# Streamed weights in two rings of buffers: six places for the split parts and four for the raw tiles, instead of five and six

## The chip, the cores and the metric

The kernel runs on one core of a Trainium2 chip. The metric is the device time of one execution in microseconds. The kernel computes in single precision on a batch of one with 256 tokens of width 1024, and it reads every weight matrix once from memory.

## The reference, cut to what matters

The reference is a network of two blocks on x of shape (1, 256, 1024). Every matrix product below is done with streamed weights, and these products are nearly all the work.

```python
# first block, layer 0: retention, 4 heads, chunks of 128
z = rms_norm(x) @ ret_w_in                  # 1024 x 6144: q, k, v, gate
o = retention(rope(q), rope(k), v)
y = (silu(gate) * rms(o)) @ ret_w_out       # 2048 x 1024
x = x + rms_norm(y);  x = x + (p[0] @ ple_w_proj[0]) * sigmoid(x @ ple_w_gate[0])
# layer 1: latent attention, 16 heads
z = rms_norm(x) @ mla_w_in                  # c_q, c_kv, k_rope, gate
s = softmax(causal(q(c_q @ w_uq) . k(c_kv @ w_uk, k_rope)))
y = (silu(gate) * (s @ (c_kv @ w_uv))) @ mla_w_out
x = x + rms_norm(y);  x = x + (p[1] @ ple_w_proj[1]) * sigmoid(x @ ple_w_gate[1])
# second block: convolution and pooling branches, then a gated feed-forward
mod = silu(c) @ w_ada + b_ada               # 1024 x 6144, on VectorE
h = layer_norm(x) * (1 + sc1) + sh1;  proj = h @ w_in
mix = (sig(gate_a) * branch_a + sig(gate_b) * branch_b) @ w_out
x = layer_norm(ALPHA * x + g1 * mix)
up = causal_dwconv((layer_norm(x) * (1 + sc2) + sh2) @ w_up)   # 1024 x 5632
x = layer_norm(ALPHA * x + g2 * (gelu(gt) * v) @ w_down)       # 2816 x 1024
```

## The kernel before, in words

All activations stay in the core's memory, transposed, with the 256 tokens as the columns of a matmul. Weights are packed ahead of time into 258 tiles of 128 x 1024 single-precision numbers (512 KB), in the order in which the program asks for them, and streamed.

**A split tile.** TensorE takes single precision at full speed only in a reduced form, so most tiles are split in two. `fetch` (L157) issues the load of a raw tile on SP's queue. `load` (L170) casts it on ScalarE into a high part (L178, tag `wh`) and subtracts that from the raw tile on VectorE, which gives the low part (L179, tag `wl`). `mm` (L236) then makes each product of three matmuls: high by high (L237), high by low (L238) and low by high (L239). A tile of 1024 columns holds eight 128-column weight blocks, or two 512-column ones where the weights are the moving operand (the value projections and the down projection).

**A plain tile.** In four places of the second block the raw tile goes to TensorE as it is, in full precision (`mm32`, L242, with its matmul on L243). `fetch` puts such a tile into a raw buffer or into a `wh` buffer, by the parity of its number. The first tile of the program is a plain one too.

**The rings.** The pool `wp` has three tags: `raw`, `wh` and `wl`. A buffer of a tag is free when the last instruction that uses its tile has ended: for a raw tile that is the subtraction on VectorE, for the parts the last matmul. A load waits on SP for a free raw buffer, a cast on ScalarE for a free `wh` buffer, a subtraction on VectorE for a free `wl` one. The scheduler of the kernel language gives out the buffers when the program is built, orders each engine's instructions by its own estimate of when they can run, and sets the waits; on the chip each engine keeps that order.

**The order of work.** `Seq` (L144) walks a list of weight blocks and calls `load` whenever a new tile begins. In the attention layer four such sequences are open at a time (`seq_g`, `seq_q`, `seq_k`, `seq_v`: gates, queries, keys, values), so that tiles of them can be half used at a time. Side work is put into the matmul stream by a clock that counts matmul columns (`tick`, `after`): softmax, normalisation, the convolution, and `ada` (L413), the 48 products that make `mod`, whose 512 KB tiles are loaded on SP's queue as well, behind one another in program order. `keep_in_program_order` is also set for the loads of the first tiles.

Of the kernel before, what the change touches and what calls it, by code (L numbers as in the profile page):

```python
# [12 lines left out]
F32R = mybir.dt.float32r  # L13
# [6 lines left out]
P = 128  # L20
S = 256
D = 1024
# [60 lines left out]
def tile_kernel(ctx, tc, order, xT, pT, pos, vec, cst, cv, rows, wada, wts, outT):  # L83
# [5 lines left out]
    wp = ctx.enter_context(tc.tile_pool(name="wp", bufs=5))  # L89
# [7 lines left out]
    def nm(s):  # L97
        uid[0] += 1
        return f"{s}_{uid[0]}"
# [44 lines left out]
    class Seq:  # L144
# [3 lines left out]
        def next(self):  # L148
            per = D // self.w
            s = self.i % per  # L150
            if s == 0:
                self.h, self.l = load(self.e[self.i:self.i + per], self.w, self.parts, self.ready.pop(0) if self.ready else None)
            self.i += 1
            sl = slice(s * self.w, (s + 1) * self.w)
            return self.h[:, sl], self.l[:, sl]

    def fetch(entries, width, parts=True, step=D, pinned=False):  # L157
        g = len(order)
        order.append((width, list(entries)))
        n = len(entries) * width  # L160
        tag, bufs = (("raw", 6), ("wh", 5), ("wl", 5))[0 if parts else [0, 1][g % len([0, 1])]]
        raw = wp.tile([P, D], F32, tag=tag, name=nm("raw"), bufs=bufs)
        for o in range(0, n, step):
            e = min(n, o + step)
            d = nc.sync.dma_start(out=raw[:, o:e], in_=wts[g, :, o:e])
            if pinned:
                tc.keep_in_program_order(d)
        return raw[:, :n]

    def load(entries, width, parts=True, raw=None):  # L170
        if raw is None:
            raw = fetch(entries, width, parts)
        if not parts:
            return raw, raw
        n = raw.shape[1]
        hi = wp.tile([P, D], F32R, tag="wh", name=nm("wh"), bufs=5)[:, :n]
        lo = wp.tile([P, D], F32R, tag="wl", name=nm("wl"), bufs=5)[:, :n]
        A.copy(hi, raw)  # L178
        V.tensor_sub(lo, raw, hi.bitcast(F32))  # L179
        return hi, lo  # L180
# [81 lines left out]
    for q in range(3):  # L262
        v0raw.append(fetch(v0[2 * q:2 * q + 2], 512, q >= 1, 512 if q == 0 else D, True))
        if q < 2:
            load_x(q + 1)
        if q == 1:
            load_x(3)
# [135 lines left out]
    def ada_steps():  # L403
        def fetch(n):
            ch = sp.tile([P, D], F32, tag="ada1", name=nm("adach"), bufs=2)
            tc.keep_in_program_order(nc.sync.dma_start(out=ch, in_=wada[n * P:(n + 1) * P, :]))
            return ch

        have = [fetch(0), fetch(1)]
        yield  # L410
        for n in range(48):
            ch = have.pop(0)
            V.tensor_tensor_reduce(ch, ch, sc, 1.0, 0.0, MUL, ADD, mod[:, n:n + 1])  # L413
            if n + 2 < 48:
                have.append(fetch(n + 2))
            if n % 8 == 7:
                m = slice(n - 7, n + 1)
                V.tensor_add(mod[:, m], mod[:, m], col("b_ada_2", n - 7, 8))
            yield
# [1087 lines left out]
```

## Time and profile before

| what | value |
|---|---|
| three runs | 850.41, 846.5, 850.07 us; median 850.07 |
| profiled execution, own time | 847.85 us |
| its span, first to last instruction | 846.1 us |
| TensorE busy | 826.1 us (98%), 6114 matmuls |
| VectorE busy | 703.1 us (83%) |
| ScalarE busy | 555.2 us (66%) |
| memory read | 165.41 MB, 197 GB/s over the span |
| mean granted TensorE clock | 0.997 |

Times are in microseconds unless marked ns. A matmul's busy time overlaps that of the next one, so a group's sum can exceed the span. A wait is put down to whoever ended it last. Engines are named PE (TensorE), PEld (its weight loads), DVE (VectorE), ACT (ScalarE), POOL (GpSimd) and SP (SyncE); a small q behind a name is the engine's sequencer, which issues DMAs.

### The profile page before, as it was taken

The page shows a single profiled execution, that of the slowest core. Times are in us where ns is not written, and L with a number is a line of the kernel's source. Part 1 is how long each engine was busy: PE and PEld are TensorE (multiplying, and loading weights), DVE is VectorE, ACT ScalarE, POOL GpSimd, SP SyncE. Part 2 cuts the span into 40 slices and gives each one's busy share as a digit, 9 for nine tenths or more (in the row PEclk, how much of TensorE's full clock was granted, in tenths as well). Part 3 has the DMA queues.
Part 4 walks back from the last instruction along what each step waited for, and adds up shares of the span by engine and source line. Part 5 has one row for each costly group of instructions (what it writes and reads, how often), then busy time and mean ns, then how long its engine had stood idle before and what let it go on. Part 6 is the DMA issues. An engine that isn't in the chain of part 4 may idle for free.

```text
span 846.1 us, 15771 instructions
## 1 busy us (share of the span) xinstructions
PE 826.1 (98%) x6114; PEld 787.9 (93%) x6114; DVE 703.1 (83%) x1283; ACT 555.2 (66%) x968; POOL 9.9 (1%) x30
## 2 busy tenths in 40 slices
PE   8999999999999999998999999999999999999995
PEld 6989999999999989998999999999998999999885
DVE  6999798988889978688874768899677888889986
ACT  7655565545676686777754857999756576666550
POOL 0000000000000000000000000000000000000001
PEclk9999999999999999999999999999999999999998
DMA  9875567778556637374255364245463455567722
GB/s 335 323 258 212 215 217 269 255 264 319 171 182 248 223 145 259 116 263 145 99 184 176 121 224 152 98 150 199 148 224 128 134 190 191 184 214 255 277 77 75
DMA packets 46634, 167.48 MB, mean 198 GB/s; under 512 B 5216, under 2 KB 5472, under 8 KB 46560
## 3 DMA queue, kind: packets, MB, share of 16 engines
q1 hardware_dynamic: 45936, 164.38, 55.1%
q0 software_dynamic: 624, 2.10, 0.9%
q8 instruction: 48, 0.79, 0.4%
q14 instruction: 26, 0.21, 0.1%
HBM read 165.41 MB, written 1.05 MB: 197 GB/s over the span
## 4 chain that ended last, share of the span: by engine, by line
PE 50%; DVE 2%; ACT 1%; issue 1%; DVEq 0%
PE ps L238 13%; PE ps L237 13%; PE ps L239 13%; PE ps L243 10%; PE ps L341 1%; PE ps L363 0%; DVE wl L179 0%; PE ps L920 0%; PE ps L1170 0%; DVE t L1434 0%; DVE sm L1415 0%; DVE half L690 0%; DVE t L1411 0%; DVE t L1412 0%; PE ps L1407 0%
## 5 line engine op out<-in xcount | busy, mean ns | idle before, releaser
L237 PE MATMUL ps<-half,wh 128*128 128x256 f32 x1504 | 425.4, 284 | 1.4 <-ACT half L187 1.4
L238 PE MATMUL ps<-half,wh 128*128 128x256 f32 x1504 | 423.8, 282 | 0.6 <-DVE half L188 0.5
L239 PE MATMUL ps<-half,wl 128*128 128x256 f32 x1504 | 422.0, 281 | 1.1 <-DVE wl L179 1.0
L178 ACT CAST wh<-raw 128x1024 fp32r<-128x1024 f32 x233 | 243.5, 1049 | 154.9 <-PE ps L238 94.8
L179 DVE TENSOR_TENSOR wl<-raw,wh 128x1024 fp32r<-128x1024 f32 x233 | 282.7, 1219 | 59.5 <-ACT wh L178 57.3
L239 PEld LDWEIGHTS ps<-half,wl 128*128 128x128 f32 x1504 | 283.8, 189 | 1.7 <-DVE wl L179 1.7
L238 PEld LDWEIGHTS ps<-half,wh 128*128 128x128 f32 x1504 | 283.4, 188 | 1.9 <-DVE half L188 1.0
L237 PEld LDWEIGHTS ps<-half,wh 128*128 128x128 f32 x1504 | 282.5, 188 | 2.6 <-ACT half L187 2.0
L243 PE MATMUL ps<-half,raw 128*128 128x256 f32 (+2 forms) x384 | 84.9, 380 | 0.0
L243 PEld LDWEIGHTS ps<-half,raw 128*128 128x128 f32 x384 | 72.5, 190 | 10.0
L237 PE MATMUL ps<-wh,half 128*128 128x512 f32 (+1 forms) x202 | 72.6, 360 | 0.9 <-ACT wh L178 0.9
L413 DVE CUSTOM_DVE_ANT_0 adach<-adach,siluc 128x1024 f32<-128x1024 f32 x48 | 58.4, 1218 | 16.7 <-DMA adach<-in_wada 16.7
L238 PE MATMUL ps<-wl,half 128*128 128x512 f32 (+1 forms) x202 | 71.0, 351 | 0.5 <-DVE wl L179 0.5
L239 PE MATMUL ps<-wh,half 128*128 128x512 f32 (+1 forms) x202 | 71.0, 352 | 0.0
L1087 ACT ACTIVATE t<-apad,vec 128x256 f32<-128x256 f32 x106 | 44.3, 501 | 0.5 <-DVE half L1088 0.5
L237 PEld LDWEIGHTS ps<-wh,half 128*128 128x128 f32 x202 | 37.9, 188 | 6.8 <-ACT wh L178 1.7
L238 PEld LDWEIGHTS ps<-wl,half 128*128 128x128 f32 x202 | 38.1, 189 | 6.0 <-DVE wl L179 1.0
L239 PEld LDWEIGHTS ps<-wh,half 128*128 128x128 f32 x202 | 38.0, 188 | 5.6
L1088 DVE TENSOR_TENSOR half<-half,t 128x512 f32<-128x512 f32 x53 | 36.5, 689 | 3.7 <-ACT t L1087 1.8
L187 ACT CAST half<-t 128x256 fp32r<-128x256 f32 (+1 forms) x47 | 20.3, 453 | 17.9 <-DVE t L1347 10.9
L188 DVE TENSOR_TENSOR half<-t,half 128x256 fp32r<-128x256 f32 (+1 forms) x47 | 21.7, 482 | 4.5 <-ACT half L187 3.6
L1342 ACT ACTIVATE t<-ps,vec 128x256 f32<-128x256 f32 x38 | 21.0, 558 | 2.0 <-PE ps L239 1.2
(290 smaller groups left out, 908.1 us busy)
## 6 DMA issues: line engine op xcount, KB each, us to landing
raw<-in_wts SPq DMA_DIRECT2D x257, 512.0 KB, 4.1
adach<-in_wada SPq DMA_DIRECT2D x48, 512.0 KB, 5.0
half<-in_xT SPq DMA_DIRECT2D x4, 256.0 KB, 5.7
half<-in_rows POOLq DMA_DIRECT2D x2, 512.0 KB, 4.7
out<-t SPq DMA_DIRECT2D x4, 256.0 KB, 2.0
cst<-in_cst SPq DMA_DIRECT2D x1, 928.0 KB, 10.6
raw<-in_wts SPq DMA_DIRECT2D x2, 256.0 KB, 4.4
siluc<-in_cv SPq DMA_DIRECT2D x1, 512.0 KB, 9.0
```

The source lines that it names most:

```text
L178: A.copy(hi, raw)
L179: V.tensor_sub(lo, raw, hi.bitcast(F32))
L187: A.copy(hi, src)
L188: V.tensor_sub(lo, src, hi.bitcast(F32))
L237: T.matmul(ps, l[0], r[0], start=first, stop=False)
L238: T.matmul(ps, l[0], r[1], start=False, stop=False)
L239: T.matmul(ps, l[1], r[0], start=False, stop=last)
L243: T.matmul(ps, w, r, start=first, stop=last)
L413: V.tensor_tensor_reduce(ch, ch, sc, 1.0, 0.0, MUL, ADD, mod[:, n:n + 1])
L1087: A.activation(t[:, b, :], apad[:, i0 + b, k:k + S], AF.Copy, scale=w[b])
L1088: V.tensor_add(acc.pair(i0 // 2), acc.pair(i0 // 2), t)
L1342: A.activation(t[:, b, :], ps[:, b, :], AF.Identity, bias=col("b_dw_f_2", m), scale=w[2])
```

## The change

The numbers of buffers of the three tags are changed, in the two functions where they stand: `raw` from 6 to 4, `wh` and `wl` from 5 to 6 each. The sum stays 16 tiles. Nothing else is edited.

```diff
-        tag, bufs = (("raw", 6), ("wh", 5), ("wl", 5))[0 if parts else [0, 1][g % len([0, 1])]]
+        tag, bufs = (("raw", 4), ("wh", 6), ("wl", 6))[0 if parts else [0, 1][g % len([0, 1])]]
         raw = wp.tile([P, D], F32, tag=tag, name=nm("raw"), bufs=bufs)
...
-        hi = wp.tile([P, D], F32R, tag="wh", name=nm("wh"), bufs=5)[:, :n]
-        lo = wp.tile([P, D], F32R, tag="wl", name=nm("wl"), bufs=5)[:, :n]
+        hi = wp.tile([P, D], F32R, tag="wh", name=nm("wh"), bufs=6)[:, :n]
+        lo = wp.tile([P, D], F32R, tag="wl", name=nm("wl"), bufs=6)[:, :n]
         A.copy(hi, raw)
         V.tensor_sub(lo, raw, hi.bitcast(F32))
```

## Rows read from the trace of the kernel before

**Rows 1.** The page, part 1: busy us, share of the span, instructions

```profile
PE 826.1 (98%) x6114; PEld 787.9 (93%) x6114; DVE 703.1 (83%) x1283; ACT 555.2 (66%) x968; POOL 9.9 (1%) x30
```

**Rows 2.** Windows: stretch, length, busy us (instructions) by engine, clock, DMA share, GB/s

```profile
20.00:40.00 20.00, 20.00 (x163) 19.64 (x162) 19.93 (x38) 13.26 (x17) 0.00 (x0) 1.00 0.88 335
...
700.00:720.00 20.00, 20.00 (x172) 20.00 (x171) 17.05 (x29) 12.85 (x21) 0.00 (x0) 1.00 0.52 185
```

**Rows 3.** Waits of PE, whole span: us in total, times, longest

```profile
PE ps L920 <- DVE sm L909: 2.8, 3, 1.7
...
PE ps L239 <- DVE wl L179: 1.0, 2, 0.7
...
PE ps L237 <- ACT wh L178: 0.9, 1, 0.9
...
PE ps L238 <- DVE wl L179: 0.5, 1, 0.5
...
PE ps L363 <- DVE t L300: 0.2, 1, 0.2
```

**Rows 4.** Waits of SP's queue, whole span

```profile
SPq L165 <- DVE wl L179: 380.4, 148, 11.6
```

**Rows 5.** Waits of ACT, whole span

```profile
ACT wh L178 <- PE ps L238: 94.8, 75, 5.0
```

**Rows 6.** Groups by line: shapes, count, busy us, mean ns, idle before, releasers

```profile
L179 DVE TENSOR_TENSOR wl<-raw,wh 128x1024 fp32r<-128x1024 f32 x233 | 282.7, 1219 | 59.5 <-ACT wh L178 57.3
...
L178 ACT CAST wh<-raw 128x1024 fp32r<-128x1024 f32 x233 | 243.5, 1049 | 154.9 <-PE ps L238 94.8 <-issue 28.1 <-PE ps L239 23.3
```

**Rows 7.** Timelines of ACT, DVE and PE near 305 us: start, us, what, [idle before]

```profile
302.71 1.03 ACT L178 CAST wh<-raw 128x1024 fp32r<-128x1024 f32 x1
...
303.77 1.23 DVE L179 TENSOR_TENSOR wl<-raw,wh 128x1024 fp32r<-128x1024 f32 x1 [0.19 <-ACT wh L178]
...
305.06 0.39 PE L239 MATMUL ps<-half,wl 128*128 128x256 f32 x1 [0.73 <-DVE wl L179]
...
308.40 0.39 PE L239 MATMUL ps<-half,wl 128*128 128x256 f32 x1 [0.24 <-DVE wl L179]
```

**Rows 8.** Waits of the weight loads, 296 to 318 us

```profile
PEld ps L239 <- DVE wl L179: 1.4, 2, 0.9
```

**Rows 9.** The raw tiles, 680 to 760 us: idle before them, landing time

```profile
  PE ps L238: 17.0, 15
...
DMA to landing us min/median/max: 3.3/3.5/4.3
```

**Rows 10.** The raw tiles, 0 to 45 us

```profile
DMA to landing us min/median/max: 3.8/6.9/10.9
```

**Rows 11.** Timelines of SP, ACT and DVE near the start

```profile
9.12 1.05 SPq L165 DMA_DIRECT2D raw<-in_wts  x2
...
14.26 1.05 ACT L178 CAST wh<-raw 128x1024 fp32r<-128x1024 f32 x1 [0.45 <-DMA raw<-in_wts]
...
14.43 1.22 DVE L179 TENSOR_TENSOR wl<-raw,wh 128x1024 fp32r<-128x1024 f32 x1
```

**Rows 12.** The raw tiles, 176 to 212 us

```profile
L179 DVE TENSOR_TENSOR wl<-raw,wh x13: 1215/1217/1226, 180.8 to 209.3; 128x1024 fp32r<-128x1024 f32 x13
...
  DMA raw<-in_wts: 2.9, 2
...
DMA to landing us min/median/max: 4.1/5.4/7.1
```

**Rows 13.** The chain of waits: the longest run of plain matmuls

```profile
533.21 27.63 PE ps L243 x128
```

**Rows 14.** Timeline of ACT at 388 us

```profile
388.76 1.05 ACT L178 CAST wh<-raw 128x1024 fp32r<-128x1024 f32 x1 [1.98 <-issue]
```

**Rows 15.** Windows, seven stretches of 20 us from 260 to 400: their sum

```profile
sum 140.00, PE 133.84 PEld 131.25 DVE 116.33 ACT 102.99 POOL 0.20; mean PE 19.12 PEld 18.75 DVE 16.62 ACT 14.71 POOL 0.03
```

## The prediction

> **What bounds the kernel now.** I read the page's busy shares first: TensorE is busy for 98% of the span [rows 1]. In a stretch with nothing but weight streaming, 700 to 720 us, it is busy 20.00 of 20.00 us at a granted clock of 1.00, the higher of its two levels, with 172 matmuls, 116 ns each [rows 2]. The reader is to see there that no buffer can add anything: TensorE has its next tile every time it asks.
>
> So I looked for what TensorE ever waits for. Its waits add up to 10.8 us in eleven rows, from 2.8 for the softmax scaling down to 0.2; split weight parts hold 1.0, 0.9 and 0.5 of them [rows 3]. TensorE's idle time is 846.1 - 826.1 = 20.0 us [rows 1]; most of what the waits leave is the last stretch, where the output is normalised. The 0.9 and the 0.5 lie at the very start (10 to 12 us), where the first tile comes from memory and nothing can run ahead. The 1.0 is at 305 and 308 us, and is the one weight stall in mid-kernel.
>
> Then who holds whom. SP issues a load when a raw buffer is free, and it waits for the splitting subtraction 380.4 us in all, 148 times [rows 4]: the raw buffers are always full. The cast on ScalarE in turn waits for matmuls 94.8 us, 75 times [rows 5]: the split buffers are full too. Both rings run ahead of TensorE; the change moves places from the outer one to the inner one.
>
> **The change part by part.**
>
> *No instruction is added or removed.* 233 casts of 1049 ns, 233 subtractions of 1219 ns [rows 6] and 259 loads of raw tiles (the first comes in two) stay. What moves is when a tile's load, cast and subtraction may begin, and with that where the scheduler puts them in the order of SP, ScalarE and VectorE.
>
> *Split parts, 5 to 6.* In steady streaming one tile feeds 8 x 3 matmuls, 24 x 116 ns = 2.79 us [rows 2]. A sixth place lets every cast run one such period earlier relative to its use, while casts still come once a period, when TensorE frees a place. It pays only where a tile was split late, and that is at 305 and 308 us: the cast comes at 302.71, the subtraction at 303.77, and the matmul on the low part at 305.06 after 0.73 us idle; the next such pause is 0.24 at 308.40 [rows 7]. ScalarE spent the time before that cast on softmax work. With a place more each of these casts would take the turn of the cast ahead of it, before the softmax. The gain is 1.0 us by the matmuls' idle time [rows 3] and 1.4 by the weight loads' [rows 8]; I take -1.3, nearer to the loads, since a weight load held up holds its matmul. The other end is 0, if the build puts those casts behind the softmax again.
>
> *Raw tiles, 6 to 4, in streaming.* A place is held from the issue of its load until its subtraction ends. Landing takes a median of 3.5 us in 680 to 760 us, 4.3 at most [rows 9]; cast and subtraction take 1.05 + 1.22 us [rows 6]. With six places a load goes out up to six periods ahead, and 6 x 2.79 - 2.3 - 3.5 = 10.9 us remain before its cast is due. With four it is 4 x 2.79 - 2.3 - 3.5 = 5.4 us. Cost: nothing, covered by those 5.4 us. Without them (landings over 8.9 us), what is late comes out of the split ring's lead, some five periods or 14 us, before TensorE feels it.
>
> *Raw tiles where loads are slow, the start.* At 20 to 40 us the queues move 335 GB/s at a share of 0.88, and VectorE is busy for 19.93 of 20.00 [rows 2]. Landing takes a median of 6.9 us up to 45 us, 10.9 at most [rows 10]. With four places the seventh load needs the subtraction that ends at 14.43 + 1.22 = 15.65, where it now goes out second in the pair from 9.12 to 10.17 [rows 11]: 5.8 us later. Its neighbours shift by less. The landing shifts less than the issue, as up to two tiles fewer are queued ahead (2 x 512 KB at 335 GB/s, 3.1 us): 5.8 - 3.1 = 2.7 us. From below the cost is 0, the split lead being at least the tile in use, 2.79 us; from above it is the whole 5.8. I take +0.4, near the lower end, because a cast there waits for its load already, 0.45 at 14.26 [rows 11], without TensorE waiting after 12 us.
>
> *Raw tiles at 176 to 212 us* (the end of the first output projection). Landing has a median of 5.4 us, 7.1 at most; the 13 subtractions lie (209.3 - 180.8) / 12 = 2.4 us apart; ScalarE waits 2.9 us, in two waits, for loads even with six places [rows 12]. Four leave 4 x 2.4 - 2.3 - 5.4 = 1.9 us, and 0.2 with the slowest landing; where a subtraction is itself late, less than nothing. The cost lies between 0 and the two periods taken, 4.8 us. I take 0: no wait of TensorE for a split part falls here [rows 3], and VectorE's backlog, not the load, sets when tiles are ready.
>
> *The plain tiles* (not split, 24 of them) alternate between the raw and the split-high ring: 2 x 4 = 8 ahead instead of 2 x 5 = 10. Such a tile is 16 matmuls of 27.63 / 128 us, 3.5 us [rows 13], so eight are 28 us ahead of loads of 3.5 to 5. Cost 0.
>
> [...]
>
> **Sum.** -1.3 + 0.4 + 0 = -0.9 us against the profiled execution, 847.85 us (span 846.1 and 1.75 around it). That run lies 2.2 below the median of the three, 850.07, so I forecast 850.07 - 0.9 = 849.2 us: no change that can be told. A measurement of this kernel tells some 0.5%, 4.25 us, from no change.
>
> **The rivals.**
>
> *Raw loads late, slower.* ScalarE works in order: the cast at 388.76 began after 1.98 us idle [rows 14], and all behind it stood as well. If casts wait for loads in the new order, the start costs up to 5.8 and the stretch at 200 us up to 4.8, and softmax and norm work behind those casts is late too. Half of both, 2.9 + 2.4, and one more stall like the largest kind in the trace, 1.7 [rows 3], make +7.0: 857. It decides once a landing exceeds four periods less 2.3 us: 8.9 us in streaming, 7.3 at 200 us. For it: 2.9 us of such waits exist with six places [rows 12], and landings of 10.9 occur [rows 10]. Against: the streaming stretches, most of the kernel, have 5.4 us to spare.
>
> [...]
>
> *The attention's pauses go too, faster.* Between 260 and 400 us TensorE is idle for 140.00 - 133.84 = 6.16 us [rows 15]. There the weights for queries, keys, values and gates run in streams of their own, each of which can keep a half-used tile, so that five places are few; with a sixth, earlier splits would leave ScalarE and VectorE free when the softmax comes. All but 1 us of it, and the start's +0.4, make -4.8: 845.3. Against: casts still come at one for each place that TensorE frees, so the same queue forms with a later tile in it.
>
> *The build reorders, and the lead does nothing.* The order on three engines is made anew from the places that are free, and stalls like those of rows 3 may come or go by 1 to 3 us each, while the 1.3 is not gained: 847 to 853, on either side of 850.5. This is the change not doing what it says.
>
> **How the numbers follow.** The forecast 0.42 and the reordering 0.18, both within the bound; the slower rival 0.22, the faster 0.18. So: faster by over 0.5% 0.18, within it 0.60, slower 0.22. The range takes in most of the faster rival and the lower half of the slower one: 844 to 857.
>
> **What would show it.** Right: in 680 to 760 us casts still wait for matmuls and not for loads; the wait for a low part at 305 us is gone; TensorE's waits in all stay within 3 us of 10.8. Wrong to the slow side: casts wait for loads far beyond the 2.9 us, and matmuls for split parts, at 20 to 45 or 190 to 215 us. Wrong to the fast side: the 6.16 us idle at 260 to 400 fall under 2. A new stall of several microseconds anywhere else would mean that the order, not the lead, decides.

## The result, and the profile after

The changed kernel takes 859.10 us (median of 4 runs, 858.58 to 862.14), the kernel before 850.24 beside it (846.50 to 850.85): a ratio of 1.0121, 95% interval 1.0083 to 1.0158. (The ratios in this document are estimates from all runs and not quotients of the two medians; that quotient is 1.0104 here.) It is slower, 10 us from the forecast and outside the range. Its profiled execution took 859.29 us, 11.4 more than that of before, which had been 2.4 us faster than its kernel's median.

Page of the kernel after, part 1 (busy us, share, instructions), to set beside [rows 1]:

```profile
PE 831.8 (97%) x6114; PEld 791.8 (92%) x6114; DVE 703.4 (82%) x1283; ACT 553.7 (65%) x968; POOL 10.2 (1%) x30
```

TensorE has the same 6114 instructions. Its idle time grew from 20.0 to 857.5 - 831.8 = 25.7 us, and its busy time by 5.7 us, for part of the work ran at a lower granted clock: 0.83 at 10 to 20 us, 0.91 at 200 to 220 and 0.66 at 830 to 840, where the kernel before has 1.00. Its waits (us in total, times, longest), for [rows 3], and ScalarE's, for [rows 5]:

```profile
PE ps L237 <- ACT half L187: 6.0, 3, 4.8
PE ps L341 <- DVE t L331: 4.1, 2, 3.5
PE ps L237 <- ACT wh L178: 1.4, 1, 1.4
...
PE ps L238 <- DVE wl L179: 0.7, 2, 0.5
```

```profile
ACT wh L178 <- PE ps L238: 76.3, 64, 3.0
ACT wh L178 <- DMA raw<-in_wts: 42.3, 23, 9.0
```

The reader is to see two things. The wait for a low part at 305 us (`L239 <- DVE wl L179`) is gone, as forecast. And ScalarE's casts, which waited 3.6 us for loads in all, now wait 42.3 us; but the two waits that grew most are TensorE's for something else, a split of an activation (L187) and a norm's square (L331). These are the instructions that stand behind such a cast in the order of ScalarE, or need what stands there.

**The largest pause, at the end.** POOL, SP, ACT, DVE and PE of the kernel after, one timeline each (start, us, what, [idle before and what ended it]):

```profile
818.68 0.91 POOL L1394 DMA_DIRECT2D g<-mod  x1 [25.38 <-DVE mod L418]
829.74 0.55 POOL L1390 DMA_DIRECT2D half<-g  x1 [10.15 <-DMA g<-mod]
```

```profile
820.64 0.33 SPq L165 DMA_DIRECT2D raw<-in_wts  x1
```

```profile
832.06 1.04 ACT L178 CAST wh<-raw 128x1024 fp32r<-128x1024 f32 x1 [9.05 <-DMA raw<-in_wts]
833.01 0.40 ACT L187 CAST half<-t 128x256 fp32r<-128x256 f32 x1
```

```profile
819.35 1.22 DVE L179 TENSOR_TENSOR wl<-raw,wh 128x1024 fp32r<-128x1024 f32 x1
...
833.13 1.23 DVE L179 TENSOR_TENSOR wl<-raw,wh 128x1024 fp32r<-128x1024 f32 x1 [8.03 <-ACT wh L178]
```

```profile
828.24 0.40 PE L239 MATMUL ps<-wh,half 128*128 128x512 f32 x1
833.46 0.80 PE L237 MATMUL ps<-wh,half 128*128 128x512 f32 x1 [4.83 <-ACT half L187]
```

Read from below. TensorE stands for 4.83 us, not for a weight but for the split of the last feature block (833.01), which stands on ScalarE behind the cast at 832.06; VectorE had that split's input ready at 823.55 + 0.42 = 823.97 (`t`, L1347). That cast waited 9.05 us for the last load of the kernel. With four raw places this load could go out only after the subtraction of 819.35 to 820.57; in the kernel before, the last load left at 807.1 and was done by 812. In between, at 818.68, POOL had issued the write of `g` (the last gate, 1024 numbers) to memory: 4 KB, which the program lays out as 1024 separate elements of 4 bytes. The load, issued 2 us later, landed after 11.3 us. The landing times (from issue to landing) of the raw tiles at 780 to 850 us (5.1 at most in the kernel before), and the traffic at 814 to 836 us in 40 slices of 0.55 us:

```profile
DMA to landing us min/median/max: 3.4/4.5/11.3
```

```profile
GB/s 357 402 335 246 30 0 0 0 0 0 0 7 0 67 52 0 0 0 37 97 37 15 22 45 30 22 7 30 97 52 156 253 156 313 201 119 97 0 0 0
```

From the 14th slice (821 us) the load is the only large transfer, and it crawls at 0 to 97 GB/s for 17 slices, until the write is done near 829.7; the first four slices show 246 to 402. After the pause TensorE ran at a mean granted clock of 0.66 for 10 us, part of them at 0.50, the lower of the two levels that its windows of 1 us show (0.50 from 832 to 838 us, 1.00 from 839): a matmul of 512 columns shows 0.63 us at 837.14 and 0.40 at 840.42 (the columns of [rows 2]):

```profile
830.00:840.00 10.00, 6.38 (x19) 4.88 (x20) 3.64 (x5) 2.63 (x3) 0.29 (x1) 0.66 0.25 74
```

**The second, at 205 to 210 us,** at the place of [rows 12]. The raw tiles at 176 to 212 us: what the casts waited for, and the landing:

```profile
  DMA raw<-in_wts: 10.6, 5
  DVE mod L413: 4.4, 1
...
DMA to landing us min/median/max: 3.6/5.4/6.7
```

Landing is as before, 5.4 us; the casts wait 10.6 us for it instead of 2.9. The 4.4 us that the profile puts down to `mod` are a wait for a load as well, as ScalarE's and SP's timelines show:

```profile
204.44 1.05 ACT L178 CAST wh<-raw 128x1024 fp32r<-128x1024 f32 x1 [4.35 <-DVE mod L413]
```

```profile
195.83 3.48 SPq L406 DMA_DIRECT2D adach<-in_wada  x2
199.41 16.10 SPq L165 DMA_DIRECT2D raw<-in_wts  x9
```

The load of that cast's tile left at 199.41, 5.0 us before the cast. It could not leave earlier, since it stood on SP behind two loads of modulation weights, which wait for VectorE (`mod`, 4.7 us in the two). The squares of the norm stand behind these casts on ScalarE, and TensorE waits 3.5 us for what follows from them (`L341 <- DVE t L331`), where it waited 1.1 us before. Behind this pause, too, the granted clock fell, to a mean of 0.91; the kernel before and the kernel after:

```profile
200.00:220.00 20.00, 18.65 (x149) 18.06 (x148) 18.20 (x31) 15.81 (x30) 0.00 (x0) 1.00 0.66 239
```

```profile
200.00:220.00 20.00, 16.48 (x120) 15.85 (x119) 14.20 (x23) 11.71 (x23) 0.00 (x0) 0.91 0.75 263
```

**Where it gained.** The seven windows from 260 to 400 us, their sum, for [rows 15]:

```profile
sum 140.00, PE 138.12 PEld 135.95 DVE 118.26 ACT 107.56 POOL 0.21; mean PE 19.73 PEld 19.42 DVE 16.89 ACT 15.37 POOL 0.03
```

TensorE's idle time there fell from 6.16 to 1.88 us.

**The account.** For every matmul I took the time to the start of the next, less the median for its line and shape, and summed what is over 0.05 us; pauses and matmuls at the lower clock both count. Us by stretch, of the profiled executions (those of the experiments are used below; 700 to 820 us shows nothing):

| kernel (raw places, split places) | 0-40 | 40-180 | 180-260 | 260-400 | 400-500 | 500-700 | 820- | sum |
|---|---|---|---|---|---|---|---|---|
| before (6, 5) | 3.5 | 2.4 | 3.3 | 10.3 | 2.6 | 1.9 | 0.4 | 24.5 |
| after (4, 6) | 5.1 | 2.5 | 6.4 | 5.2 | 2.5 | 6.1 | 8.2 | 36.0 |
| e1 (4, 5) | 2.4 | 2.6 | 6.7 | 6.3 | 3.9 | 2.2 | 9.2 | 33.3 |
| e4 (4, 6), `g` early | 3.4 | 5.9 | 9.1 | 5.7 | 2.6 | 7.5 | 0.4 | 34.8 |
| e5 (4, 6), `g` by TensorE | 3.3 | 2.5 | 6.7 | 5.2 | 2.4 | 7.0 | 0.4 | 27.6 |
| e10 (4, 5), `g` by TensorE | 3.5 | 2.6 | 10.5 | 7.5 | 4.0 | 2.2 | 0.4 | 30.7 |
| e7 (6, 5), `g` early | 3.3 | 2.4 | 2.6 | 13.2 | 2.6 | 2.0 | 0.4 | 26.7 |
| e6 (6, 5), `g` by TensorE | 3.4 | 2.5 | 2.1 | 15.7 | 2.8 | 2.0 | 0.4 | 28.9 |
| e2 (5, 6) | 3.9 | 2.4 | 4.4 | 8.4 | 2.4 | 2.4 | 0.4 | 24.4 |
| e8 (5, 6), `g` by TensorE | 3.4 | 2.4 | 2.0 | 9.5 | 2.4 | 2.4 | 0.4 | 22.6 |
| e9 (5, 5) | 3.4 | 3.4 | 3.8 | 5.8 | 2.4 | 2.0 | 0.4 | 21.3 |

36.0 - 24.5 = 11.5 us, the whole difference of these two executions (the medians lie 8.9 apart): +7.8 at the end, +4.2 at 500 to 700 us (same pattern, casts that wait 12.0 us for loads at 580 to 660), +3.1 near 200, +1.6 at the start, where this execution had the lower clock for a few us, as another execution here had (e10, 0.87 at 0 to 10 us), and -5.1 in the attention.

Each row is one execution, and executions with the same rings differ. In the attention the three with six and five places show 10.3, 13.2 and 15.7 us; at 280 to 300 us the granted clock was 1.00 in the first and 0.91 in the other two. At 180 to 260 us e1 and e10 show 6.7 and 10.5. So a difference of a few microseconds in one column counts only where several rows bear it out. They do at the end, at 500 to 700 us, near 200 us (6.4 to 10.5 in the five rows with four raw places, 2.1 to 3.3 in the three with six and five) and in the attention for four raw places against six and five (5.2 to 7.5, 10.3 to 15.7).

### The profile page after: what moved, and what is told of

It is laid out like the page before. It is cut to its first block, busy times and chain, and to the rows that moved or that the text cites. A ratio compares the mean times of both kernels' runs of the same rounds, so it can differ in the third digit from the quotient of the medians.

```text
span 857.5 us, 15781 instructions
## 1 busy us (share of the span) xinstructions
PE 831.8 (97%) x6114; PEld 791.8 (92%) x6114; DVE 703.4 (82%) x1283; ACT 553.7 (65%) x968; POOL 10.2 (1%) x30
## 4 chain that ended last, share of the span: by engine, by line
PE 65%; DVE 15%; DMA 10%; ACT 6%; issue 3%; SPq 0%; DVEq 0%; ACTq 0%
PE ps L238 20%; PE ps L239 19%; PE ps L237 19%; DMA raw<-in_wts 6%; DVE wl L179 4%; DMA adach<-in_wada 4%; PE ps L243 4%; DVE half L1088 2%; ACT wh L178 2%; DVE adach L413 1%; PE ps L341 1%; PE ps L363 1%; DMA half<-in_xT 1%; ACT t L1087 1%; PE ps L920 1%
## 5 line engine op out<-in xcount | busy, mean ns | idle before, releaser
L239 PE MATMUL ps<-half,wl 128*128 128x256 f32 x1504 | 421.9, 281 | 0.0
L179 DVE TENSOR_TENSOR wl<-raw,wh 128x1024 fp32r<-128x1024 f32 x233 | 283.1, 1220 | 67.1 <-ACT wh L178 64.8
L239 PEld LDWEIGHTS ps<-half,wl 128*128 128x128 f32 x1504 | 283.7, 189 | 0.0
L237 PE MATMUL ps<-wh,half 128*128 128x512 f32 (+1 forms) x202 | 74.0, 367 | 6.2 <-ACT half L187 4.8
L239 PE MATMUL ps<-wh,half 128*128 128x512 f32 (+1 forms) x202 | 72.3, 358 | 0.0
L239 PEld LDWEIGHTS ps<-wh,half 128*128 128x128 f32 x202 | 38.7, 192 | 5.8
L187 ACT CAST half<-t 128x256 fp32r<-128x256 f32 (+1 forms) x47 | 20.4, 453 | 17.2 <-DVE t L1347 10.4
```

What stands on the lines that cost most here:

```text
L187: A.copy(hi, src)
L237: T.matmul(ps, l[0], r[0], start=first, stop=False)
L239: T.matmul(ps, l[1], r[0], start=False, stop=last)
```

## The experiments

The theory: two raw places fewer are the loss, because loads then go out so late that casts wait for them, and ScalarE, working in order, holds what TensorE needs. The rival: the sixth split place remakes the order, and that is the loss. Kernels of one group ran beside the same runs of the kernel before (851.11 us for e1 to e4, 852.41 for e5 to e8, 851.42 for e9 to e12). Of the edits only what matters is shown.

**e1.** One half of the change:

```diff
-... (("raw", 6), ("wh", 5), ("wl", 5)) ...
+... (("raw", 4), ("wh", 5), ("wl", 5)) ...
```

> Raw ring 4, split rings left at 5. Theory A (the two raw places taken are the loss: casts wait for loads and hold ScalarE, and the last raw load goes out so late that it runs into the scattered write of g2): slower than before by as much as the changed kernel or more, since the attention's gain of some 4 us needs the sixth split place: 859 to 864; casts wait for loads over 30 us in all, the last load lands over 8 us after its issue, TensorE stands 4 to 6 us for it. Rival B (the sixth split place remakes the order on VectorE, and that is the loss): 849 to 852, the last load lands in under 5 us.

862.48 us, ratio 1.0144 (1.0110 to 1.0178): the whole loss, without a sixth split place. The end is the same, a landing of 11.3 us included (TensorE stands 6.5 us there, 4.8 in the kernel after), and the wait at 305 us (`L239`, 1.0 us) is back.

**e2** and **e3.** The sixth split place with five and with six raw ones. There is no room for either as it stands. e2 drops two unused tiles (`cosT`, `sinT`) and lets `krs` share a buffer; e3 also takes one head's decay mask for all four heads, so it leaves three masks out and loads less at the start.

```diff
+... (("raw", 5), ("wh", 6), ("wl", 6)) ...   # e2
+... (("raw", 6), ("wh", 6), ("wl", 6)) ...   # e3
...
-    cosT = cp.tile([P, S], F32, name="cosT")
-    sinT = cp.tile([P, S], F32, name="sinT")
```

> Raw ring 5, split rings 6, one tile more than before or after; the room comes from two small unused tiles and one that shares its place with another. Theory A: the one raw place given back ends most of the loss: the last load goes out one subtraction earlier, about 6 us before the write of g2, and lands in under 5 us; casts wait for loads 10 to 20 us in all; the attention's gain stays: 846 to 851. Rival B: the order stays as in the changed kernel: 856 to 860.

> Raw ring left at 6, split rings 6: the other half of the change by itself. The room comes as in the run before, and from keeping the decay mask of one head instead of four (all heads use that one, and the constants' load is 352 KB instead of 928). Theory A: casts wait for loads under 5 us in all; no loss left, the attention's pauses shrink by 3 to 5 us: 843 to 848. Rival B (the sixth split place is the loss): 854 to 860.

e2: 848.63 us, 0.9980 (0.9956 to 1.0004). e3: 846.64, 0.9949 (0.9930 to 0.9968). The rival falls: the loss is there without a sixth split place (e1), and a kernel with one isn't slower than before where five or six raw places stay. How much of e3's 0.5% is the smaller masks' is not shown.

**e4.** Is the end stall the scattered write? The write is moved from 819 to 96 us, by taking the first eight columns of `mod` in place of the last gate's, which this kernel so leaves out; the order on the other four engines is the same as in the kernel after.

```diff
-    nc.gpsimd.dma_start(out=g2.rearrange("(k p) -> p k", p=P), in_=mod[:, 40:48])
+    nc.gpsimd.dma_start(out=g2.rearrange("(k p) -> p k", p=P), in_=mod[:, 0:8])
```

> The changed kernel, but g2 is written from eight columns of mod that are ready long before (the final gate is therefore the wrong one): the scattered write leaves the end, and nothing else changes on TensorE, VectorE, ScalarE and SP. Theory A' (the last raw load was slow because it ran beside that write): its landing falls from 11.3 to 4 to 6 us, TensorE's stall of 4.8 at 828 us and the slower clock behind it go: faster than the changed kernel by 5 to 7.5 us, 851.5 to 854. Rival (the load was slow for another reason, or was late by itself): 857 to 860.

858.36 us, 1.0094 (1.0067 to 1.0122): a miss, some 4 us more than expected. The end did as expected (0.4 instead of 8.2 in the table, the clock stays at 1.00). The cost went with the write. POOL, the raw tiles' landing and the traffic of e4 at 88 to 120 us (slices of 0.8 us):

```profile
95.94 1.06 POOL L1394 DMA_DIRECT2D g<-mod  x1 [93.79 <-DVE mod L418]
```

```profile
DMA to landing us min/median/max: 3.6/6.0/13.1
```

```profile
GB/s 220 189 312 399 353 302 348 61 0 10 82 246 299 111 92 36 26 31 56 36 56 26 26 41 123 333 389 405 420 420 435 399 348 343 333 200 241 282 92 102
```

From the 14th to the 24th slice (98 to 107 us), with three loads of raw tiles and one of modulation weights on their way, the queues move 26 to 111 GB/s. The casts behind them wait, and 3.4 us are lost at 100 to 120 us, where the kernel after loses 0.1. The loss near 200 us is larger too (9.1 against 6.4), but e10 below has 10.5 there without any such write, so that part isn't shown to be the write's. The slow load itself is shown a second time, at another place, with the same write in front of it.

**e5** and **e6.** No scattered write at all: `g` is spread over the partitions by eight small matmuls and two copies, and the load of its row goes with the write; e5 does it in the kernel after, e6 in the kernel before.

```diff
-    nc.gpsimd.dma_start(out=g2.rearrange("(k p) -> p k", p=P), in_=mod[:, 40:48])
-    g2r = row(g2)
+    for n in range(2):
+        pb = bank()
+        for k in range(4):
+            c = 40 + 4 * n + k
+            T.matmul(pb[:, k * P:(k + 1) * P], mod[:, c:c + 1].to_broadcast([P, P]), ident, start=(k == 0), stop=(k == 3))
+        A.copy(g2r[:, 512 * n:512 * n + 512], pb)
```

> The kernel after, with the scattered write of g and its row load replaced by eight broadcast matmuls on TensorE and two copies, so that no DMA with 4-byte elements runs at all. Theory (two raw places are lost; the largest single loss is a load caught behind the scattered write): no raw landing over 8 us anywhere, the end stall of 4.8 us and the slow clock after it are gone, as in e4, and nothing is lost at 100 us, where e4 lost it; minus 7.7 us, plus about 1.7 us for the added matmuls: 852.5 to 854.5, ratio to before 1.002 to 1.005, so still no faster than before, because the pauses near 200, 600 and 640 us stay. Rival (four raw places stall the end by themselves, whatever the write does): a raw landing or a cast's wait over 4 us remains after 820 us, 858 to 861. Rival (the whole loss is the write): 848 to 850.

> The kernel before with the same replacement, as the control for it. Theory: with six raw places the write hides behind 9 us of spare in the loads, so nothing is won by removing it: 850 plus 1.7 us for the matmuls, less up to 1 us of the row's wait near the end, 850 to 852, ratio 1.000 to 1.003. If the write costs the kernel before something too: 846 to 849.

e5: 854.42 us, 1.0020 (0.9999 to 1.0042). e6: 852.14, 0.9999 (0.9981 to 1.0017). Both as the theory has it: removing the write gives the kernel after 1.0% back, the added matmuls paid, and the one before nothing. e5's longest landing is 6.3 us at 45 to 140 and 6.1 from 780 on. Its last raw load leaves at the same moment as in the kernel after (820.7 us), and its casts wait 1.2 us for loads from 780 us on instead of 9.0 (who waited for the loads, and their landing):

```profile
L165 SPq DMA_DIRECT2D raw<-in_wts x13: 327/328/328, 781.8 to 820.7; - x13
...
  ACT wh L178: 1.2, 1
...
DMA to landing us min/median/max: 3.5/4.6/6.1
```

So four raw places alone make that load late, and only the write beside it makes it late enough to stop TensorE. What stays in e5 is the middle: 6.7 us at 180 to 260 and 7.0 at 500 to 700 in the table.

**e7.** The early write in the kernel before: do six raw places cover it? (Like e4, it leaves the last gate out.)

```diff
-... in_=mod[:, 40:48])
+... in_=mod[:, 0:8])
```

> The kernel before with the write of g taken from the first columns of mod, so that it runs near 95 us instead of 814 us (the output is not the reference's in this factor); the order on the four other engines is the same. Theory: raw landings of 11 to 13 us appear there as in e4, but with six raw places they are covered by a spare of about 11 us between landing and cast: under 1 us of pause between 100 and 125 us (e4: 3.4 us), time 850 to 851.5. Rival (the write stops the work itself, whatever the number of raw places): 3 us or more of pause there, 853 to 854.

850.25 us, 0.9979 (0.9953 to 1.0004). The write went out at 94.35 us and loads beside it slowed, though the longest landed in 9.0 us, less than the 11 to 13 that I expected:

```profile
DMA to landing us min/median/max: 3.6/5.6/9.0
```

TensorE lost 0.1 us at 100 to 120 us, e4 3.4. The write by itself doesn't stop TensorE. How much of the difference is the spare of six places, and how much the shorter landing (9.0 us against 13.1), these two runs don't separate.

**e8.** Five raw, six split places (e2) with `g` by TensorE as in e5:

> Five raw places and six split ones (as e2) with g by TensorE. Theory: e2's 848.6 with nothing to win from the write (its last loads land in 5 us already): 848 to 850.5, ratio 0.997 to 1.000. If the write costs something here: 845 to 847, the best of all that fit.

850.05 us, 0.9974 (0.9950 to 0.9997). Against e5 it has one raw place more, in the room that e2 freed, and the middle is healed: 2.0 against 6.7 us at 180 to 260, 2.4 against 7.0 at 500 to 700. (e2, the same rings with the write, shows 4.4 and 2.4.) The wait for the square near 200 us is gone; casts wait for loads 6.4 us in all instead of 46.8. Over all the kernels TensorE's wait for this square is 0 to 1.3 us with six raw places, 0 to 2.5 with five and 3.2 to 7.2 with four, and only behind the waits of four places is the mean granted clock at 200 to 220 us 0.83 to 0.91; elsewhere it is 0.98 or more.

**e9** and **e10.** One raw place fewer and nothing else; and four raw places without the write or a sixth split place.

```diff
+... (("raw", 5), ("wh", 5), ("wl", 5)) ...   # e9
+... (("raw", 4), ("wh", 5), ("wl", 5)) ...   # e10, with e5's g
```

> Five raw places, five split ones: one place fewer in the raw ring and nothing else. Theory (the loss lies where the spare between landing and cast runs out): one place takes about 3 us of the 11 us of spare in streaming and leaves 2 to 3 us near 200 us and at the end, so under 1.5 us is lost, all near 200 us: 850.5 to 852.5, ratio 1.000 to 1.003. Rival (each place costs the same, half of e1's 1.4%): 856, ratio 1.007.

> Four raw places, five split ones, g by TensorE. Theory: e1's 1.4% less the end stall (about 0.9%), that is the pauses in mid-kernel alone, without what the sixth split place wins in attention: ratio 1.004 to 1.008, and e5's 1.002 against it is the sixth place's gain. Rival (the sixth place wins nothing beside four raw ones): 1.001 to 1.003, as e5.

e10: 855.08 us, 1.0033 (1.0013 to 1.0054), just under the theory's 1.004, and not told apart from e5. e9 is a miss: 847.92 us, 0.9957 (0.9935 to 0.9978), faster than before, where I expected a small loss. It still waits near 200 us (1.9 us for the square), but the pauses of the attention went, as in the kernel after. So did the wait at 305 us, with five split places. TensorE's longest waits in e9 and its windows from 260 to 400 us (1.72 us idle):

```profile
PE ps L341 <- DVE t L331: 2.0, 2, 1.9
PE ps L243 <- DMA raw<-in_wts: 1.4, 1, 1.4
PE ps L276 <- DVE eps_l L280: 1.1, 1, 1.1
```

```profile
sum 140.00, PE 138.28 PEld 135.74 DVE 119.19 ACT 105.23 POOL 0.21; mean PE 19.75 PEld 19.39 DVE 17.03 ACT 15.03 POOL 0.03
```

**e11** and **e12.** Six raw places and a sixth for one of the split rings, in the room that e2 freed:

```diff
+... (("raw", 6), ("wh", 6), ("wl", 5)) ...   # e11
+... (("raw", 6), ("wh", 5), ("wl", 6)) ...   # e12
```

> Six raw places, six for the upper parts, five for the lower ones; it needs the two unused tiles that e2 dropped. If the casts' wait for a free upper place (94.8 us of it in the kernel before, all on the release by the matmuls) is what the sixth place relieves, this has e3's gain or most of it: 845.5 to 848.5, ratio 0.993 to 0.998. If both rings are needed, since the subtraction behind the cast waits for a lower place: 849 to 852, ratio 0.999 to 1.001.

> Six raw places, five for the upper parts, six for the lower ones, the counterpart of e11. If the upper ring is what is short: ratio 0.999 to 1.001, and the casts wait for the matmuls as before. If the lower ring is: 0.993 to 0.998, and e11 shows no gain.

851.36 us, 1.0009 (0.9989 to 1.0029), and 850.19, 0.9995 (0.9977 to 1.0013). A sixth place in one of the two rings alone gains nothing that can be told. With both (e3) there may be a gain, but e3 also has the smaller masks, so it is not shown. Where the sixth split place is all that differs (the kernel after and e1; e5 and e10; but for the unused tiles, e2 and e9), the intervals overlap.

## Why the prediction was wrong

*Raw tiles, 6 to 4, in streaming: the size was right, the cover was not.* The 5.4 us between landing and cast are there: at 680 to 780 us the median is 5.4 us in the kernel after (11.1 before), and the casts at 680 to 760 still wait for matmuls, never for loads, the landing being 3.5 us as in [rows 9]. What failed is the next clause, that a landing over 8.9 us would come out of the split ring's lead, 14 us, before TensorE feels it. One landing of 11.3 us came, and TensorE stood for 4.83 us, because the cast that waited was in front of other work on ScalarE. A lead in weights doesn't cover work that is no weight. I had the mechanism as a rival, from [rows 14], though that row names no load as what the cast waited for; the rows at 832.06 and 833.01 do. I priced its places at the start and near 200 us. That the price of 857 came near is luck: in the account those places cost 4.7 us of its 7.0 (and at the start it was the clock), places that I had not named cost 12.0, and the attention gave 5.1 back. The largest of them, the last load of the kernel beside the write of `g`, I did not look at. I took landing times from 680 to 760 us, 0 to 45 and 176 to 212, and none from the stretch with the odd transfer in it. e1 against e10, four raw places with and without the write: 1.0144 against 1.0033.

*Raw tiles at 176 to 212 us: "I take 0" failed.* The loss is +3.1 us in the account, 3.5 in TensorE's wait, within the bounds of 0 to 4.8. My reason was that no wait for a split part fell there in [rows 3]. The waits that came are for the norm behind the casts, with the granted clock lower after them (0.91). Such waits came at 500 to 700 us too, 4.2 us in the account, a stretch that the prediction did not price at all; e8 against e5 shows that one raw place heals both, and e2 against the kernel after bears it out (4.4 against 6.4 us near 200, 2.4 against 6.1). At 500 to 700 us it takes four raw places together with six split ones (6.1 to 7.5 us in the table; 2.2 in e1 and e10): with a larger split ring than raw ring a cast can stand in ScalarE's order long before its load is there. That reading is argued from the waits, not tested, and it can't be the whole of it: e2 and e8, with six split places on five raw ones, show 2.4 us there.

*Split parts, 5 to 6: the wait went, but that the sixth place took it is not shown.* The wait at 305 us is gone in the kernel after, e4 and e5, and there in e1 and e10. But it is gone in e9 too, with five split places, and 0.2 and 0.3 us of it stay in e2 and e8, with six: the order made anew from the places can do it as well. In the attention the sixth place makes 6.3 to 5.2 (e1 to after) and 7.5 to 5.2 (e10 to e5), 1.1 and 2.3 us, for my 1.3; beside five raw places it makes 5.8 to 8.4 and 9.5 (e9 to e2 and e8), the other way. That is within what executions of the same rings differ by, so my 1.3 is neither borne out nor refuted. In the time of the whole kernel it can't be told.

*The attention's pauses: the fast rival's sign was right, its cause wrong.* They fell by 5.1 us, under the 2 us idle that I had named, but most of it came with fewer raw places: 10.3 to 6.3 in e1 and to 5.8 in e9, both with five split places, and e9's gain shows in the kernel's time (0.9957). e2 and e8, with five raw and six split places, show 8.4 and 9.5. Why fewer raw tiles ahead leave ScalarE and VectorE freer for the softmax stays open; the order of the three engines is another one, and I have no run that separates the order from the places. That *the build reorders* holds for this stretch. The sign that I had named for it, a new stall of several microseconds elsewhere, came at 828 us, but e4 has the order of the kernel after on TensorE, ScalarE, VectorE and SP and no such stall: that one was the late load.

*The start and the plain tiles: right as nothing.* The first 40 us show 2.4 to 3.5 us in e1, e4, e5 and e10, all with four raw places, and 3.5 before; what the kernel after shows more there (5.1) goes with its granted clock of 0.83 at 10 to 20 us. TensorE's wait for plain tiles in the kernel after is 0.4 us, as before.

So one raw place fewer gained 0.4%, the second cost 1.9% (0.9957 to 1.0144): about 1.1% of that the write's (e1 to e10), the rest, as far as the account shows, the casts in mid-kernel. The bounds near 200 us held. The sum was wrong, because I put nothing where TensorE showed no wait yet: 12.0 us came at the end and at 500 to 700 us, to which the prediction gave no cost. e9, one raw place fewer, beats both kernels.

## What to carry to other kernels

Here the ring of load buffers had to be sized by its worst landing, so look for that landing where another transfer runs beside the loads, down to the last one; the median in steady streaming says how far the ring can shrink only there. When a load is late, ask what stands behind its first reader in that engine's order, for TensorE may wait for that and not for the load. And take a ring down in single steps: here the first step gained and the second lost four times as much.

## What the runs showed of the hardware

The product of a 128 x 128 weight block with 256 columns took TensorE 20.00 us / 172 = 116 ns in the reduced form of single precision [rows 2], and 27.63 us / 64 = 432 ns in full precision (128 matmuls in the profile, 16 for the eight blocks of a tile [rows 13]). What other forms take, no run shows.

A write of 4 KB, which the program lays out in 4-byte pieces (32 packets in the profile of e4), took 10.5 us to land in the kernel after, 11.8 in e4, and 9.0 in the kernel before, there with no load beside it; the 512 KB load of its row behind it took 5.1 (after) and 4.3 (before). While it was on its way, with loads of SP's queue in flight beside POOL's write, the queues moved 0 to 97 GB/s (after) and 26 to 111 (e4); right after it they moved 333 to 435 in e4. Four executions show it: raw loads of 512 KB took 11.3 us (after, e1), 13.1 (e4) and 9.0 (e7), where the medians are 3.5 in streaming and 5.4 near 200 us, and the one other place with landings over 9 us is the start [rows 10]. It is not POOL's queue as such: two loads of 512 KB that POOL issued at 788 us in the kernel before landed in 4.7 us (median), with raw landings from 780 us on of 5.1 at most. That the small pieces are what counts, and not the writing, is not shown; no run writes `g` in larger ones. In the kernel before nothing was in flight at that moment (0 to 8 GB/s from 814 to 824 us, the write's own), and taking the write out gained nothing that can be told (e6, ratio 0.9999).
